# Hybrid decoder layer on one core: attention scores and linear attention rewritten with products of 128 rows and one state per pair of heads

## The chip, the cores and the metric

The kernel runs on one core of a Trainium2 chip. The metric is the device time of one execution in microseconds (us); 0.5% of it is 10 us.

## What is computed

One decoder layer over 1024 tokens of width 1024, in float32. One input projection feeds two head groups; their outputs go through one output projection, and a mixture of 32 experts with 4 chosen per token follows. The change touches the two head groups alone:

```python
# (A) window attention: 8 query heads, 2 key heads, width 64, blocks of 128 tokens with the block before
s = einsum('bnqhgd,bnkhd->bnhgqk', qb, kb) * scale        # masked, softmax with a sink, times v

# (B) linear attention: 4 heads, key width 64, value width 128, chunks of 64 tokens
glog = log_sigmoid(ga @ w_gla_gate_up + b_gla_gate) / 16
b = cumsum(g, axis=2); b_last = b[:, :, -1:]; b_mid = b[:, :, C // 2 - 1:C // 2]
A = einsum('bnihd,bnjhd->bnhij', q * exp(b - b_mid), k * exp(b_mid - b))     # causal inside a chunk
o = einsum('bnhij,bnjhv->bnihv', A, v)
kv = einsum('bnjhd,bnjhv->bnhdv', k * exp(b_last - b), v)
state = exp(b_last) * state + kv                                             # chunk after chunk
o = o + einsum('bnihd,bnhdv->bnihv', q * exp(b), states)                     # the state before the chunk
```

## The kernel before

The program is written with tiles and pools; a scheduler sets the order of the instructions on each engine, which the engines then keep. It has three stages. The first (to about 165 us) normalises the tokens and makes queries, keys and gate inputs for all 1024 tokens; `pieces_of_k` (L359 to L366) writes the float16 key `kk`, twice over 128 partitions for each key head, and its remainder `kl` (L365), in 64 partitions for each key head. The second, the mixer, is the loop over t = 0 to 7 of `layer_kernel` (from L675), each pass over a tile of 128 tokens, that is two chunks of 64. The third (router, experts, output) begins with `project_out`.

In pass t, SP loads pieces of the output weights (`wo`, L684 and L687) and of `w_ada` (L634); GpSimd reduces the latter (`ada_half`, L636 to L643). `project` (L149 to L151 inside it) makes values and output gates with 96 float16 products of 256 columns; they depend on nothing in the pass, and the scheduler strews them among the others as filling on TensorE. `gla_gates` (L532 to L563) makes the decay factors: one product of 16 rows (L535), a bias added by VectorE (L537), ScalarE's logarithm (L539 to L541), a running sum by a product with a triangle (L546), four tiles of exponentials (L552 to L557) and four multiplications of 256 columns (L562). `attention` makes its scores with 16 products (L466 and L467): for each of 8 heads one of 128 rows with the key and one of 64 rows with the remainder:

```python
nc.tensor.matmul(pss[g][:, a, :w], qq[:, g, i, tq], kk[:, g, tk], start=True, stop=False)
nc.tensor.matmul(pss[g][:, a, :w], qq[g * 64:(g + 1) * 64, g, i, tq],
                 kl[g * 64:(g + 1) * 64, tk], start=False, stop=True)
```

VectorE masks and reduces each head (L472). The pool `psS` has two buffers, so the scores of the second four heads wait until L472 has read those of the first. After L472 come the softmax (L476 to L486), transposes (L493) and 16 products with the values (L502). `gla` makes the chunk products (L570, 64 rows each), selects the causal part of both chunks (L573), transposes the keys (L576), then for each chunk four products of 64 by 64 (L589) and a new state (L593), and for each head one product of 128 rows with the values (L600) and one of 64 rows with the state of each chunk (L603). The second chunk's state product waits for L593. L608 to L611 normalise the result `go`, which L710 transposes.

Of the kernel before, what the change touches and what calls it, by code (L numbers as in the profile page):

```python
# [19 lines left out]
T = 1024  # L20
D = 1024
NT = 8
# [27 lines left out]
def layer_kernel(  # L50
# [110 lines left out]
    kl = midp.tile([128, T], F16, name="kl")  # L161
# [3 lines left out]
    gaT = midp.tile([16, T], F32, name="gaT")  # L165
# [6 lines left out]
    with tc.tile_pool(name="p1", bufs=1) as p1, tc.tile_pool(name="stage", bufs=4) as stage, \  # L172
# [210 lines left out]
        for t in range(NT):  # L383
# [8 lines left out]
            nc.vector.tensor_copy(gaT[:, tk], pt[:16, 0:128])  # L392
# [24 lines left out]
    with tc.tile_pool(name="p2", bufs=1) as p2, tc.tile_pool(name="wk", bufs=2) as wk, \  # L417
            tc.tile_pool(name="wos", bufs=1, side="right") as wos:
        wup = p2.tile([16, 256], F32, name="wup")
        nc.sync.dma_start(wup, w_up)  # L420
        bgb = p2.tile([128, 256], F32, name="bgb")
        nc.sync.dma_start(bgb, bcast_row(b_gla_gate, 256))
# [9 lines left out]
        nc.vector.tensor_scalar(amask[:, 128:256], io, 0.0, -1e30, op0=OP.is_gt, op1=OP.mult)  # L432

# [12 lines left out]
        S0 = wk.tile([128, 2, 128], F32, name="Sn", bufs=4)  # L446
        nc.vector.memset(S0, 0.0)
        Sst = [S0]
# [4 lines left out]
        def attention(t, ao):  # L453
# [4 lines left out]
            for i2 in range(2):  # L458
# [3 lines left out]
                for a in range(2):  # L462
                    for g in range(2):
# [3 lines left out]
                        nc.tensor.matmul(pss[g][:, a, :w], qq[g * 64:(g + 1) * 64, g, i, tq],  # L467
                                         kl[g * 64:(g + 1) * 64, tk], start=False, stop=True)
# [63 lines left out]
        def gla_gates(t):  # L532
# [9 lines left out]
            nc.vector.scalar_tensor_tensor(zb, zb, 0.0, az, op0=OP.min, op1=OP.subtract)  # L542
            pb = psS.tile([128, 2, 256], F32, name="pss")
            pbv = pb[:, 0, :].rearrange("p (a n) -> p a n", a=2)
            for a in range(2):
                nc.tensor.matmul(pbv[:, a, :], zb[:, a * 128:(a + 1) * 128], tri16, start=True, stop=True)  # L546
            bT = wk.tile([128, 4, 64], F32, name="bT", bufs=1)
            bf = bT.rearrange("p a n -> p (a n)")
            nc.scalar.activation(bf, pb[:, 0, :], AF.Copy)
            ee = wk.tile([128, 4, 256], F32, name="ee")  # L550
            ev = ee.rearrange("p e (a n) -> p e a n", a=4)
            nc.vector.tensor_tensor(ev[:, 0], bT, bT[:, :, 31:32].to_broadcast([128, 4, 64]), op=OP.subtract)  # L552
            nc.vector.tensor_tensor(ev[:, 2], bT[:, :, 63:64].to_broadcast([128, 4, 64]), bT, op=OP.subtract)
            nc.scalar.activation(ee[:, 1, :], ee[:, 0, :], AF.Exp, scale=-1.0)
            nc.scalar.activation(ee[:, 0, :], ee[:, 0, :], AF.Exp)
            nc.scalar.activation(ee[:, 2, :], ee[:, 2, :], AF.Exp)
            nc.scalar.activation(ee[:, 3, :], bf, AF.Exp)  # L557
            e3 = wk.tile([128, 4], F32, name="e3")
            nc.vector.tensor_copy(e3, ev[:, 3, :, 63])
# [3 lines left out]
            return qk, e3  # L563

        def gla(t, qk, e3, gv, sgg, go):
            A = am[t % 2]
            pas = [psS.tile([128, 2, 128], F32, name="pss") for _ in range(2)]
            for h in range(4):
                bs = slice(64 * (h % 2), 64 * (h % 2) + 64)
                nc.tensor.matmul(pas[h % 2][:, h // 2, :], qk[bs, 1, h // 2, :], qk[bs, 0, h // 2, :],  # L570
                                 start=True, stop=True)
            for par in range(2):
                nc.vector.copy_predicated(A[:, par::2, :], triu[:, None, :].to_broadcast([128, 2, 128]), pas[par])  # L573
            pk = psT.tile([128, 4, 128], F32, name="pt")
            for a in range(2):
                nc.tensor.transpose(pk[:, a, :], qk[:, 2, a, :], identf)  # L576
            k2 = wk.tile([128, 2, 128], F32, name="k2", bufs=1)
            nc.scalar.activation(k2, pk[:, 0:2, :], AF.Copy)
            k2f = k2.rearrange("p a n -> p (a n)")
            Sc = []  # L580
            for cch in range(2):
                Sc.append(Sst[0])
                if t == NT - 1 and cch == 1:
                    break
                cs = slice(64 * cch, 64 * cch + 64)
                pkv = psS.tile([128, 2, 128], F32, name="pss")
                for h in range(4):
                    bs = slice(64 * (h % 2), 64 * (h % 2) + 64)
                    nc.tensor.matmul(pkv[bs, h // 2, :], k2f[cs, h * 64:(h + 1) * 64],  # L589
                                     gv[cs, h * 128:(h + 1) * 128], start=True, stop=True)  # L590
                Sn = wk.tile([128, 2, 128], F32, name="Sn", bufs=4)
                for a in range(2):
                    nc.vector.scalar_tensor_tensor(Sn[:, a, :], Sst[0][:, a, :], e3[:, 2 * a + cch:2 * a + cch + 1],  # L593
                                                   pkv[:, a, :], op0=OP.mult, op1=OP.add)
                Sst[0] = Sn
            pos2 = [psO.tile([128, 2, 128], F32, name="po") for _ in range(2)]
            for h in range(4):
                bs = slice(64 * (h % 2), 64 * (h % 2) + 64)
# [878 lines left out]
```

## Time and profile before

| | |
|---|---|
| median of 3 runs | 2007.46 us (2006.25 to 2015.17) |
| profiled execution | 2014.17 us, of which the span in the trace is 2012.4 us |
| TensorE matmul busy | 1847.7 us, 92% of the span |
| VectorE / ScalarE / GpSimd busy | 1545.2 / 1303.8 / 991.0 us |
[...]

Busy time of TensorE counts a product until its modelled end, so neighbours overlap; the distance between two starts is what a product costs in a stream. A float32 product leaves two records, so "x8" there is four products. Idle time stands in brackets, with what ended it.

### The profile page before, as it was taken

The page shows a single profiled execution, that of the slowest core. Times are in us where ns is not written, and L with a number is a line of the kernel's source. Part 1 is how long each engine was busy: PE and PEld are TensorE (multiplying, and loading weights), DVE is VectorE, ACT ScalarE, POOL GpSimd, SP SyncE. Part 2 cuts the span into 40 slices and gives each one's busy share as a digit, 9 for nine tenths or more (in the row PEclk, how much of TensorE's full clock was granted, in tenths as well). Part 3 has the DMA queues.
Part 4 walks back from the last instruction along what each step waited for, and adds up shares of the span by engine and source line. Part 5 has one row for each costly group of instructions (what it writes and reads, how often), then busy time and mean ns, then how long its engine had stood idle before and what let it go on. Part 6 is the DMA issues. An engine that isn't in the chain of part 4 may idle for free. (4 is left out here: it accounts for less than half of the span.)

```text
span 2012.4 us, 55645 instructions
## 1 busy us (share of the span) xinstructions
PE 1847.7 (92%) x22929; PEld 1583.9 (79%) x22929; DVE 1545.2 (77%) x2518; ACT 1303.8 (65%) x2248; POOL 991.0 (49%) x986
## 2 busy tenths in 40 slices
PE   7999999989778999999999999999999999999980
PEld 3456767655468999999999997779889998999970
DVE  6823655666759998998999996679787978989863
ACT  5523444443447787787787885668677868968860
POOL 2204757635636455554574663336453534754442
PEclk8999989999869999999999999999999999999985
DMA  8512323243299999999999998589888989999983
GB/s 277 165 46 74 85 80 93 83 141 126 100 317 329 354 363 320 340 360 325 350 347 358 366 341 289 198 309 342 313 284 293 362 274 338 361 317 344 323 262 105
DMA packets 296773, 525.94 MB, mean 261 GB/s; under 512 B 19071, under 2 KB 79753, under 8 KB 296482
## 3 DMA queue, kind: packets, MB, share of 16 engines
q1 hardware_dynamic: 277824, 476.40, 68.2%
q0 software_dynamic: 17392, 41.72, 8.7%
q8 instruction: 181, 2.97, 0.6%
q10 hardware_dynamic: 1298, 4.21, 0.5%
q14 instruction: 78, 0.64, 0.1%
HBM read 482.50 MB, written 39.76 MB: 260 GB/s over the span
## 5 line engine op out<-in xcount | busy, mean ns | idle before, releaser
L169 DVE SCALAR_TENSOR_TENSOR el<-st,eh 128x1024 f16<-128x1024 f32 x768 | 934.8, 1239 | 92.4 <-ACT eh L168 88.4
L168 ACT ACTIVATE eh<-st 128x1024 f16<-128x1024 f32 x768 | 794.5, 1055 | 240.3 <-PE pu L150 121.5
L149 PE MATMUL pu<-xTh,eh 128*128 128x232 f16 (+31 forms) x4096 | 779.2, 231 | 9.2 <-DVE lin L1122 4.7
L151 PE MATMUL pu<-xTh,el 128*128 128x232 f16 (+31 forms) x4096 | 778.4, 230 | 5.8 <-issue 5.7
L150 PE MATMUL pu<-xTl,eh 128*128 128x232 f16 (+31 forms) x4096 | 778.1, 230 | 4.1 <-issue 3.9
L150 PEld LDWEIGHTS <-eh 128*128 128x128 f16 x6080 | 595.0, 99 | 38.8 <-issue 16.7
L149 PEld LDWEIGHTS <-eh 128*128 128x128 f16 x6080 | 592.9, 98 | 29.7 <-issue 7.7
L151 PEld LDWEIGHTS <-el 128*128 128x128 f16 x6080 | 592.4, 98 | 29.8 <-issue 7.9
L1125 POOL CAST aTh<-lin 128x232 f16<-128x232 f32 (+31 forms) x256 | 296.7, 1159 | 495.5 <-DVE lin L1124 457.3
L149 PE MATMUL pyv<-aTh,eh 128*128 128x232 f16 (+30 forms) x1984 | 375.2, 231 | 5.9 <-ACT yT L1152 4.5
L150 PE MATMUL pyv<-aTl,eh 128*128 128x232 f16 (+30 forms) x1984 | 374.8, 231 | 3.2 <-issue 3.2
L151 PE MATMUL pyv<-aTh,el 128*128 128x232 f16 (+30 forms) x1984 | 374.9, 231 | 0.8 <-issue 0.8
L1126 POOL TENSOR_TENSOR aTl<-lin,aTh 128x232 f16<-128x232 f32 (+31 forms) x256 | 255.3, 997 | 20.7
L1122 DVE TENSOR_SCALAR lin<-pu,bt 128x232 f32<-128x232 f32 (+31 forms) x256 | 109.7, 428 | 76.8 <-PE pu L151 58.0
L1167 POOL DMA_INDIRECT yacc<-yo,tokI x52 | 94.6, 1819 | 113.7 <-ACT yo L1164 107.1
L636 POOL TENSOR_TENSOR st<-st,sil 128x512 f32<-128x512 f32 x64 | 68.4, 1069 | 153.6 <-DVE ee L562 96.7
L1118 ACT ACTIVATE gl<-pu,bt 128x232 f32<-128x232 f32 (+31 forms) x256 | 98.0, 383 | 62.9 <-PE pu L151 36.6
L1123 DVE SCALAR_TENSOR_TENSOR lin<-lin,bt,sg 128x232 f32<-128x232 f32 (+31 forms) x256 | 104.5, 408 | 18.1 <-ACT sg L1120 4.2
L1120 ACT ACTIVATE sg<-gl,c 128x232 f32<-128x232 f32 (+31 forms) x256 | 107.9, 421 | 1.0
L1080 POOL DMA_INDIRECT xg<-h2d,gatI x50 | 70.8, 1416 | 43.4 <-DVE gcol L1243 21.1
L1124 DVE SCALAR_TENSOR_TENSOR lin<-gl,lin 128x232 f32<-128x232 f32 (+31 forms) x256 | 83.6, 326 | 4.3
L1072 PE MATMUL pxh<-identh,xg 128*128 128x128 f16 (+27 forms) x848 | 55.6, 206 | 19.7 <-DMA xg<-h2d,gat 11.7
(402 smaller groups left out, 2501.4 us busy)
## 6 DMA issues: line engine op xcount, KB each, us to landing
st<-in_w_mlp_dram SPq DMA_DIRECT2D x384, 1024.0 KB
st<-in_w_ada_dram SPq DMA_DIRECT2D x64, 256.0 KB
xt<-in_x_dram SPq DMA_DIRECT2D x16, 512.0 KB
st<-in_w_ada_dram SPq DMA_DIRECT2D x16, 512.0 KB
st<-in_w_in_dram SPq DMA_DIRECT2D x7, 1024.0 KB
x1d<-xt SPq DMA_DIRECT2D x8, 512.0 KB
h2d<-h2s SPq DMA_DIRECT2D x8, 512.0 KB
yacc<-yi ACTq DMA_DIRECT2D x8, 512.0 KB
```

The costliest lines, as they stand in the source:

```text
L149: nc.tensor.matmul(ps, sh, mh, start=first, stop=False)
L150: nc.tensor.matmul(ps, sh, ml, start=False, stop=False)
L151: return nc.tensor.matmul(ps, sl, mh, start=False, stop=last)
L168: return (nc.scalar.activation(dh, src, AF.Copy, scale=SW), nc.vector.scalar_tensor_tensor(dl, src, SW, dh, op0=OP.mult, op1=OP.subtract))
L169: nc.vector.scalar_tensor_tensor(dl, src, SW, dh, op0=OP.mult, op1=OP.subtract))
L1118: nc.scalar.activation(gl, pu[0], AF.Relu, scale=-SG, bias=bc(0, j))
L1120: sgs.append(nc.scalar.activation(sg, gl, AF.Sigmoid, scale=-1.702 * INV / SG, bias=c7))
L1122: nc.vector.tensor_scalar(lin, pu[1], bc(1, j), bc(2, j), op0=OP.max, op1=OP.min)
L1123: nc.vector.scalar_tensor_tensor(lin, lin, bc(3, j), sg, op0=OP.add, op1=OP.mult)
L1125: nc.gpsimd.tensor_copy(aTh[:, j, :], lin)
L1126: lows.append(nc.gpsimd.tensor_tensor(aTl[:, j, :], lin, aTh[:, j, :], op=OP.subtract))
L1167: end["dma"] = nc.gpsimd.indirect_dma_start(out=yacc, out_offset=bass.IndirectOffsetOnAxis(ap=si(b)[:m, :], axis=0), in_=yo[:m, :], in_off ...
```

## The change

The remainder `kl` gets its own copy in all 128 partitions for each key head, so all 16 score products have 128 rows (L470). The bias of the gates becomes a row of the weights `wup`, met by a row of ones in `gaT`; VectorE's addition goes, and the product has 128 rows. In `gla_gates` the state factors are written per chunk, so that a tile's two chunks share one state step: the keys of the first chunk and the queries of the second are also multiplied by the other chunk's whole decay. In `gla` there are four extra products of 64 columns (L585: second chunk's queries with first chunk's keys), copied beside the causal part (L590); one product of 128 rows and 256 columns for each pair of heads with the state `S` (L593), which holds the two heads in diagonal blocks; two products of 256 columns for the new state in place of eight (L606), and none in the last pass. The head results lie in one PSUM tile in place of two.

```diff
-    kl = midp.tile([128, T], F16, name="kl")
+    kl = midp.tile([128, 2, T], F16, name="kl")
-    gaT = midp.tile([16, T], F32, name="gaT")
+    gaT = midp.tile([128, T], F32, name="gaT")
+    nc.gpsimd.memset(gaT, 0.0)
+    nc.gpsimd.memset(gaT[32:33, :], 1.0)
...
-                nc.vector.scalar_tensor_tensor(kl[hi, ts], ps[hi], INV * SX, kk[hi, g, ts],
-                                               op0=OP.mult, op1=OP.subtract)
+                for at in (hi, lo):
+                    nc.vector.scalar_tensor_tensor(kl[at, g, ts], ps[hi], INV * SX, kk[hi, g, ts],
+                                                   op0=OP.mult, op1=OP.subtract)
...
-        wup = p2.tile([16, 256], F32, name="wup")
-        nc.sync.dma_start(wup, w_up)
-        bgb = p2.tile([128, 256], F32, name="bgb")
-        nc.sync.dma_start(bgb, bcast_row(b_gla_gate, 256))
+        wup = p2.tile([128, 256], F32, name="wup")
+        nc.vector.memset(wup, 0.0)
+        nc.sync.dma_start(wup[0:16, :], w_up)
+        nc.sync.dma_start(wup[32:33, :], bcast_row(b_gla_gate, 256, 1))
...
-                        nc.tensor.matmul(pss[g][:, a, :w], qq[g * 64:(g + 1) * 64, g, i, tq],
-                                         kl[g * 64:(g + 1) * 64, tk], start=False, stop=True)
+                        nc.tensor.matmul(pss[g][:, a, :w], qq[:, g, i, tq], kl[:, g, tk], start=False, stop=True)
...
-            zb = wk.tile([128, 256], F32, name="zb", bufs=1)
-            nc.vector.tensor_add(zb, pz[:, 0, :], bgb)
-            nc.scalar.activation(az, zb, AF.Abs)
+            nc.scalar.activation(az, pz[:, 0, :], AF.Abs)
...
-            for n, src in enumerate((gqT, gkT, gkT, gqT)):
+            for n, src in ((0, gqT), (1, gkT)):
                 nc.vector.tensor_tensor(qk[:, n], src[:, :, tk], qk[:, n], op=OP.mult)
+            for n, src, c in ((4, gkT, 0), (2, gqT, 1)):
+                for cch, to in ((c, 3), (1 - c, n)):
+                    cs = slice(64 * cch, 64 * cch + 64)
+                    nc.vector.tensor_tensor(qk[:, to, :, cs], src[:, :, t * 128 + 64 * cch:t * 128 + 64 * cch + 64],
+                                            qk[:, n, :, cs], op=OP.mult)
+                cs = slice(64 * c, 64 * c + 64)
+                nc.vector.tensor_tensor(qk[:, n, :, cs], qk[:, 3, :, cs],
+                                        e3[:, :, 1 - c:2 - c].to_broadcast([128, 2, 64]), op=OP.mult)
+            nc.vector.tensor_tensor(e4, e3[:, :, 0], e3[:, :, 1], op=OP.mult)
...
+                nc.tensor.matmul(pa[:, 0:128], qk[bs, 1, h // 2, :], qk[bs, 0, h // 2, :], start=True, stop=True)
+                nc.tensor.matmul(pa[:, 128:192], qk[bs, 3, h // 2, :], qk[bs, 3, h // 2, 64:128],
                                  start=True, stop=True)
...
+                nc.vector.tensor_copy(A[0:64, par::2, 64:128], pas[par][0:64, :, 128:192])
+            pos4 = psO.tile([128, 4, 128], F32, name="po")
+            for a in range(2):
+                nc.tensor.matmul(pos4[:, 2 * a:2 * a + 2, :].rearrange("p h n -> p (h n)"), qk[:, 2, a, :], S[:, a, :],
+                                 start=True, stop=False)
+                for h in (2 * a, 2 * a + 1):
+                    nc.tensor.matmul(pos4[:, h, :], A[:, h, :], gv[:, h * 128:(h + 1) * 128],
+                                     start=False, stop=bool(h % 2))
+            if t < NT - 1:
...
+                for a in range(2):
+                    nc.tensor.matmul(pkv[:, a, :], k2[:, a, :], gv[:, a * 256:(a + 1) * 256], start=True, stop=True)
+                for a in range(2):
+                    for hh in range(2):
+                        bs, ns = slice(64 * hh, 64 * hh + 64), slice(128 * hh, 128 * hh + 128)
+                        nc.vector.scalar_tensor_tensor(S[bs, a, ns], S[bs, a, ns], e4[bs, a:a + 1],
+                                                       pkv[bs, a, ns], op0=OP.mult, op1=OP.add)
```

The scheduler's order changes with it. On VectorE in pass t = 5, before, the first head's reduction (L472, two rows each) stands in the middle of the decay factors (`ee`):

```order
L712 SCALAR_TENSOR_TENSOR hTl<-pt,ggc,hTh 128x4x128
L552 TENSOR_TENSOR ee<-bT 128x256
L553 TENSOR_TENSOR ee<-bT 128x256
L559 COPY e_3203<-ee 128x4
L472 ISA sm,mx<-pss,amask 128x256
L472 ISA mx 128x1
L562 TENSOR_TENSOR ee<-gqT,ee 128x256
L562 TENSOR_TENSOR ee<-gkT,ee 128x256 x2
L562 TENSOR_TENSOR ee<-gqT,ee 128x256
L528 SCALAR_TENSOR_TENSOR vg_3309<-pb,vg_3309 128x512
L472 ISA sm,mx<-pss,amask 128x256
```

The same place with the change, where L474 is the reduction and L560 to L573 are the decay factors and their new pieces:

```order
L554 TENSOR_TENSOR ee<-ee 128x256
L563 TENSOR_TENSOR ee<-gkT,ee 128x256
L567 TENSOR_TENSOR ee<-gkT,ee 128x2x64 x2
L563 TENSOR_TENSOR ee<-gqT,ee 128x256
L560 COPY e_3171<-ee 128x4
L567 TENSOR_TENSOR ee<-gqT,ee 128x2x64
L570 TENSOR_TENSOR ee<-ee,e_3171 128x2x64
L567 TENSOR_TENSOR ee<-gqT,ee 128x2x64
L570 TENSOR_TENSOR ee<-ee,e_3171 128x2x64
L573 TENSOR_TENSOR e_3181<-e_3171 128x2
L527 TENSOR_SCALAR vg_3283<-vg_3283 128x512
L474 ISA sm,mx<-pss,amask 128x256
```

No reduction now comes before the last decay factor. On TensorE the scores move to match: in pass 5, before, the first eight score products follow L546 at once and 30 projection products stand between them and the next four; now 34 projection products stand between L546 and the first eight, and 8 behind them.

On TensorE at the end of pass 5, before, the states and the results of the last two heads come last, between the last projection products and the next pass:

```order
L150 LDWEIGHTS hTh
L150 MATMUL pb<-wvl_1329,hTh 128x256
L589 MATMUL pss<-vg_3258,k_3476 64x128 x8
L151 LDWEIGHTS hTl
L151 MATMUL pb<-wvh_1328,hTl 128x256
L603 MATMUL po<-Sn,ee 64x128 x2
L600 MATMUL po<-vg_3258,am_1386 128x128
L603 MATMUL po<-Sn,ee 64x128 x2
L600 MATMUL po<-vg_3258,am_1386 128x128
L603 MATMUL po<-Sn,ee 64x128 x2
```

With the change the results of all four heads (L593 and L596) stand earlier, among the transposes (L495) and the products with the values (L504) of the attention:

```order
L495 MATMUL pt<-identf,sm 128x128 x5
L593 MATMUL po<-S,ee 128x256
L596 MATMUL po<-vg_3232,am_1392 128x128 x2
L593 MATMUL po<-S,ee 128x256
L504 MATMUL po<-vv,pT 128x64 x8
L495 MATMUL pt<-identf,sm 128x128 x4
L596 MATMUL po<-vg_3232,am_1392 128x128 x2
```

The new state's two products (L606) stay at the end of the pass, and no product of the pass waits for the state they make.

## Rows read from the trace of the kernel before

**Rows 1.** The page: span, busy time, and granted clock in 40 slices.
```profile
span 2012.4 us, 55645 instructions
...
PE 1847.7 (92%) x22929; PEld 1583.9 (79%) x22929; DVE 1545.2 (77%) x2518; ACT 1303.8 (65%) x2248; POOL 991.0 (49%) x986
...
PEclk8999989999869999999999999999999999999985
```
**Rows 2.** Windows: start:end, length, busy PE, PEld, DVE, ACT, POOL, clock, DMA share, GB/s.
```profile
164.00:420.00 256.00, 242.19 (x1859) 175.88 (x1857) 147.82 (x419) 117.28 (x374) 163.58 (x261) 0.97 0.32 92
...
650.00:2000.00 1350.00, 1271.56 (x18749) 1196.35 (x18746) 1149.94 (x1539) 1005.70 (x1529) 684.55 (x598) 0.98 0.94 319
```
**Rows 3.** Timeline of TensorE in pass 5 (start, duration, instruction): scores, projections, transposes.
```profile
331.39 0.68 PE L546 MATMUL pss<-tri,zb 128*128 128x128 f32 x4 [0.59 <-DVE zb L542]
331.91 0.27 PE L466 MATMUL pss<-kk,qq 128*128 128x256 f16 x1
...
333.61 0.28 PE L150 MATMUL pb<-wvl,hTh 128*128 128x256 f16 x1
...
333.84 0.27 PE L149 MATMUL pb<-wvh,hTh 128*128 128x256 f16 x1
333.95 0.27 PE L150 MATMUL pb<-wvl,hTh 128*128 128x256 f16 x1
...
342.39 0.38 PE L493 MATMUL pt<-identf,sm 128*128 128x128 f32 x2
342.61 0.27 PE L150 MATMUL pb<-wvl,hTh 128*128 128x256 f16 x1
```
**Rows 4.** Waits: total us, times, longest; weight loads of L467.
```profile
PEld L467 <- issue: 11.2, 30, 2.4
```
**Rows 5.** Timeline of TensorE in pass 5: linear attention, and L502 between.
```profile
339.90 0.71 PE L570 MATMUL pss<-ee 64*128 64x128 f32 x4
340.55 0.28 PE L149 MATMUL pb<-wvh,hTh 128*128 128x256 f16 x1
...
343.99 1.10 PE L502 MATMUL po<-vv,pT 128*128 128x64 f32 x8
344.93 0.72 PE L493 MATMUL pt<-identf,sm 128*128 128x128 f32 x5
345.49 0.39 PE L600 MATMUL po<-vg,am 128*128 128x128 f32 x2
345.80 0.43 PE L603 MATMUL po<-Sn,ee 64*64 64x128 f32 x2
346.16 0.28 PE L151 MATMUL pb<-wvh,hTl 128*128 128x256 f16 x1
...
353.74 0.68 PE L589 MATMUL pss<-vg,k 64*64 64x128 f32 x16
354.35 0.28 PE L151 MATMUL pb<-wvh,hTl 128*128 128x256 f16 x1
354.84 0.43 PE L603 MATMUL po<-Sn,ee 64*64 64x128 f32 x4 [0.21 <-DVE Sn L593]
...
356.78 0.69 PE L535 MATMUL pss<-wup,gaT 16*128 16x256 f32 x2
```
**Rows 6.** Timeline of TensorE: the two longest waits of the mixer, passes 3 and 7.
```profile
270.20 0.27 PE L466 MATMUL pss<-kk,qq 128*128 128x256 f16 x1 [2.04 <-DVE mx L472]
...
420.15 0.84 PE L710 MATMUL pt<-identf,go 128*128 128x128 f32 x3 [2.28 <-DVE go L611]
```
**Rows 7.** Windows, columns as in rows 2: the stretch around the wait of pass 3.
```profile
268.00:284.00 16.00, 13.96 (x72) 9.53 (x70) 7.51 (x29) 5.34 (x19) 9.84 (x15) 0.68 0.19 56
```
**Rows 8.** Timeline of VectorE in pass 3: start of the decay factors, first reduction.
```profile
261.61 0.41 DVE L542 SCALAR_TENSOR_TENSOR zb<-zb,az 128x256 f32<-128x256 f32 x1
...
268.79 0.41 DVE L472 CUSTOM_DVE_ANT_0 sm<-pss,amask 128x256 f32<-128x256 f32 x1
```
**Rows 9.** The instructions of line L562: shortest/median/longest ns, first and last start.
```profile
L562 DVE TENSOR_TENSOR ee<-gqT,ee x16: 407/422/1281, 170.5 to 397.0; 128x256 f32<-128x256 f32 x16
```

More of the change, by code (lines that the diff above doesn't have):

```diff
@@ L391, in layer_kernel @@
             nc.tensor.transpose(pt[:16, 0:128], ga[:, t, :], identf)
[L392 removed]
+            nc.vector.tensor_copy(gaT[0:16, tk], pt[:16, 0:128])
         for base, dst, sc in ((768, gqT, INV / 8), (1024, gkT, INV)):
@@ L445, in layer_kernel @@
             am.append(a)
-        S0 = wk.tile([128, 2, 128], F32, name="Sn", bufs=4)
-        nc.vector.memset(S0, 0.0)
-        Sst = [S0]
+        S = p2.tile([128, 2, 256], F32, name="S")
+        nc.gpsimd.memset(S, 0.0)
         for i in range(2):
@@ L545, in gla_gates @@
             for a in range(2):
-                nc.tensor.matmul(pbv[:, a, :], zb[:, a * 128:(a + 1) * 128], tri16, start=True, stop=True)
-            bT = wk.tile([128, 4, 64], F32, name="bT", bufs=1)
-            bf = bT.rearrange("p a n -> p (a n)")
+                nc.tensor.matmul(pbv[:, a, :], az[:, a * 128:(a + 1) * 128], tri16, start=True, stop=True)
+            ee = wk.tile([128, 5, 256], F32, name="ee")
+            ev = ee.rearrange("p e (a n) -> p e a n", a=4)
+            bT, bf = ev[:, 2], ee[:, 2, :]
@@ L566, in gla @@
+            e4 = wk.tile([128, 2], F32, name="e4")
+            nc.vector.tensor_tensor(e4, e3[:, :, 0], e3[:, :, 1], op=OP.mult)
+            return ee, e4
+        def gla(t, ee, e4, gv, sgg, go):
             A = am[t % 2]
-            pas = [psS.tile([128, 2, 128], F32, name="pss") for _ in range(2)]
+            qk = ee.rearrange("p e (a n) -> p e a n", a=2)
+            pas = [psS.tile([128, 2, 256], F32, name="pss") for _ in range(2)]
             for h in range(4):
                 bs = slice(64 * (h % 2), 64 * (h % 2) + 64)
-                nc.tensor.matmul(pas[h % 2][:, h // 2, :], qk[bs, 1, h // 2, :], qk[bs, 0, h // 2, :],
+                pa = pas[h % 2][:, h // 2, :]
+                nc.tensor.matmul(pa[:, 0:128], qk[bs, 1, h // 2, :], qk[bs, 0, h // 2, :], start=True, stop=True)
+                nc.tensor.matmul(pa[:, 128:192], qk[bs, 3, h // 2, :], qk[bs, 3, h // 2, 64:128],
@@ L575, in gla @@
+            pos4 = psO.tile([128, 4, 128], F32, name="po")
             for a in range(2):
[L576 to L591, printed above, removed]
-                for a in range(2):
-                    nc.vector.scalar_tensor_tensor(Sn[:, a, :], Sst[0][:, a, :], e3[:, 2 * a + cch:2 * a + cch + 1],
-                                                   pkv[:, a, :], op0=OP.mult, op1=OP.add)
-                Sst[0] = Sn
@@ L596, in gla @@
-            pos2 = [psO.tile([128, 2, 128], F32, name="po") for _ in range(2)]
-            for h in range(4):
-                bs = slice(64 * (h % 2), 64 * (h % 2) + 64)
-                po = pos2[h % 2][:, h // 2, :]
-                nc.tensor.matmul(po, A[:, h, :], gv[:, h * 128:(h + 1) * 128], start=True, stop=False)
-                for cch in range(2):
-                    cs = slice(64 * cch, 64 * cch + 64)
-                    nc.tensor.matmul(po[cs, :], qk[bs, 3, h // 2, cs], Sc[cch][bs, h // 2, :],
-                                     start=False, stop=True)
+                nc.tensor.matmul(pos4[:, 2 * a:2 * a + 2, :].rearrange("p h n -> p (h n)"), qk[:, 2, a, :], S[:, a, :],
+                                 start=True, stop=False)
@@ new lines, in gla @@
+                for h in (2 * a, 2 * a + 1):
+                    nc.tensor.matmul(pos4[:, h, :], A[:, h, :], gv[:, h * 128:(h + 1) * 128],
+                                     start=False, stop=bool(h % 2))
+            if t < NT - 1:
+                pk = psT.tile([128, 4, 128], F32, name="pt")
+                for a in range(2):
+                    nc.tensor.transpose(pk[:, a, :], qk[:, 4, a, :], identf)
+                k2 = wk.tile([128, 2, 128], F32, name="k2", bufs=1)
+                nc.scalar.activation(k2, pk[:, 0:2, :], AF.Copy)
+                pkv = psS.tile([128, 2, 256], F32, name="pss")
+                for a in range(2):
[5 more added lines that the diff above has]
+                                                       pkv[bs, a, ns], op0=OP.mult, op1=OP.add)
@@ L691, in layer_kernel @@
             ao = wk.tile([128, 8, 64], F32, name="ao", bufs=1)
-            qk, e3 = gla_gates(t)
+            gates = gla_gates(t)
             gv, sgg = project(t, row)
@@ L706, in layer_kernel @@
             go = wk.tile([128, 4, 128], F32, name="go", bufs=1)
-            gla(t, qk, e3, gv, sgg, go)
+            gla(t, *gates, gv, sgg, go)
             pt = psT.tile([128, 4, 128], F32, name="pt")
```

24 lines of the change are left out of this document (10 added, 14 removed).

## The prediction

> **What bounds the kernel now.** I read the page first, for where time passes, then windows by stage, then the timeline of TensorE through one pass of the mixer, then its waits. [...] The change touches the mixer, from 164 to 420 us. There TensorE works for 242.2 of 256 us at a mean granted clock of 0.97, while VectorE is busy for 148, ScalarE for 117 and GpSimd for 164 us, and the transfers take a third of their engines' time [rows 2]. So the mixer lasts as long as TensorE's stream of products plus 13.8 us of waits. The experts follow it and run at a DMA share of 0.94 [rows 2]; their weights are not read during the mixer, so whatever the mixer gains moves the rest forward whole.
>
> **The scores.** A projection product, 128 rows and 256 columns of float16, follows another at 0.11 us (333.84 to 333.95) [rows 3]. The first eight score products of pass 5, of the same 256 columns, take 331.91 to 333.61, that is 1.70 us or 0.21 each [rows 3]. They alternate between 128 and 64 rows. Two other rows say that the alternation is what costs. The weight loads of L467 are not hidden: 30 of them stand idle for 11.2 us, 0.37 each [rows 4]. And transposes of 128 rows, of another type and put between projections, cost no extra: two in 0.22 us (342.39 to 342.61) [rows 3]. With all sixteen at 128 rows I price them at 0.11: 16 x 0.11 = 1.76 in place of 3.40 us, 1.64 less in each of passes 1 to 7, 11.5 us. Pass 0 has half the columns and no row here; between nothing and 1.6 us I take 0.8. Sum: 12.3 us less.
>
> [...]
>
> **The linear attention, per pass.** Four steps, all by rows 5.
> - Four extra products of 64 columns. In float32 and 128 rows such a product costs 0.235 us (four from 343.99 to 344.93), one of 64 rows and 128 columns 0.325 (two from 339.90 to 340.55) [rows 5]. Ends: half of 0.325, and 0.325. I take 0.235, the nearest in columns: 0.94 more (0.65 to 1.30).
> - The results. Before, a head costs 0.67 us (0.31 for L600, 0.36 for its two state products; 345.49 to 346.16), and this stands twice; the other two heads run from the end of the last projection, 354.35 + 0.11, to 356.78, 2.32 with a wait of 0.21 that I count below [rows 5]. Together 3.45 without the wait. After, four products at 0.31 and two of 256 columns in float32, for which no row stands: at most twice 0.31, at least the 0.44 that four float16 products of 256 columns need [rows 3, 5]. I take 0.5: 2.24, so 1.2 less (1.0 to 1.3).
> - The states. Eight products of 64 by 64 take 0.61 us (353.74 to 354.35), 0.08 each where one of 128 rows takes 0.31, so they run beside each other [rows 5]. Two of 256 columns at 0.5 are 1.0: 0.4 more (0.25 to 0.65). This part speaks against the change.
> - The gate product has 128 rows for 16 and the same columns: nothing, or a tenth less.
>
> Sum per pass: 0.94 - 1.2 + 0.4 = 0.14 more, 1.1 in eight; the last pass drops its states and two transposes (some 0.5 less, and the 0.4 is not paid). So 0.2 more in all, which I call nothing, with ends of 6 us less and 6 more. The linear attention is a wash; the scores carry the gain.
>
> **The waits.** The wait for the new state, 0.21 us [rows 5], stands in all eight passes: 1.7 us go, since the results now read the state of the pass before. The results stand earlier in the order, so the chain behind them (squares, root, `go`, transposes) starts earlier, and the longest wait of the mixer, 2.28 us for `go` in pass 7 [rows 6], should go too. Without the bias addition on VectorE (0.4 us and a hand-over) the gates reach L546 earlier; the wait there, 0.59 in pass 5 [rows 3], goes in the passes that have it: 1 us. What is late next are the second four heads' scores. They wait for VectorE's reduction of the first (L472 of before), and the new order puts all decay factors ahead of it. There are four half-width multiplications, two half-width scalings and a tiny product more, two full multiplications and the addition less. By columns alone this is some 0.5 us more per pass before the first reduction, at the full price of each instruction (0.42) [rows 9] 1.8 more. TensorE brings 34 + 8 projections and eight scores, 42 x 0.11 + 0.87 = 5.5 us, after L546. VectorE needs 6 to 7 us there. So I expect waits of half a microsecond to one in each of seven passes, some 5 us, where before one pass had 2.04 [rows 6] and the others at most half of that, some 3 in all: 2 us more.
>
> [...]
>
> Work I cost at nothing: the second copy of `kl` (four more instructions on VectorE, before 165 us), because TensorE has projections queued there and VectorE waits for it; the two memsets on GpSimd, idle then; the copies beside the causal part, hidden by projections up to about 0.4 us a pass, beyond which they would delay the softmax; the bias transfer, now one row. GpSimd and SP keep their work. GpSimd is busy for 164 of 256 us [rows 2] and would bind only if a pass fell well under 27 us; I expect 28 from 30.
>
> **The sum.** 12.3 + 0 + 1.7 + 2.3 + 1.0 - 2.0 is 15.3 us less on waits and products at the high clock. In the mixer the clock was at 0.97, so 3% of 256 us or 8 us were lost to the low level, and fewer long waits give back perhaps a third: 2.5. I forecast 18 us less. The profiled execution of 2014.2 us becomes 1996; it lay 6.7 above the median, so the median goes from 2007.5 to **1989.5 us**.
>
> **Rivals.**
> - *VectorE's chain takes the gain and more (slower).* In pass 3 the chain from the gates' end (261.61 + 0.41) to the first reduction took 6.8 us [rows 8], since multiplications that meet GpSimd's take up to 1281 ns for a median 422 [rows 9]. TensorE waited 2.04 us [rows 6], and the 16 us around it ran at a clock of 0.68 [rows 7]: 16 x 0.32 = 5.1 us lost, 7.2 in all. Now the chain is longer in every pass. Waits near 2 us decide, because after this one the clock fell. If five to seven of seven passes do this, it costs 36 to 50 us, less the 7 paid already and the 18 gained: 11 to 25 slower, about 2025. Three or four such passes eat the gain: 2004 to 2011. For it speaks the order; against it that before only one of seven passes did so, and that the reductions now follow each other closely. 0.08 for the slower form, 0.10 for the even one.
> - *The scores stay at 0.21 us (the change does not do what it is for).* If the price is that of accumulating two products in one place and not of the alternation, 12.3 of the 18 us fall away: 2002. Rows 4 speak against it. [...] 0.10.
> - *The clock stays high throughout the mixer.* All 8 us come back and not a third: 1984 or, with the float32 products at their low ends, 1978. For it speaks that the longest waits go; 0.12.
>
> **The numbers.** The forecast has 0.60: 1982 to 1997. Half a per cent, 10 us, is about what a measurement of this kernel can tell from no change. Faster by more than that takes the forecast and the high clock, 0.72; the same takes this even form and the scores that stay, 0.20; slower 0.08. The range for 8 in 10 runs from 1976 to 2006: it leaves out the slower rival and the ends of the others.
>
> **What would show it.** Right: score products 0.11 us apart; a pass of about 28 us where it was 30; no wait of L600's successors for the state; the eight products of L589 replaced by two of 0.4 to 0.6; the stretch after 420 us unchanged but shifted. Wrong: waits of TensorE for the reduction (L474 in the new numbering) of 2 us and more in several passes, with the clock at 0.5 behind them; score products still 0.2 apart; float32 products of 256 columns at over 0.62; the gain of the mixer not found again at the end.

## The result, and the profile after

The median is 1986.0 us (4 runs, 1980.7 to 1991.8) where the kernel before has 2011.3 beside it: a ratio of 0.987 (95% interval 0.983 to 0.992), some 25 us less. Seven more runs, taken later, gave 1985.7 beside 2009.7: 0.990 (0.987 to 0.994). The forecast was 1989.5, 18 us less, in a range of 1976 to 2006.

The page after, against [rows 1]: TensorE is busy for 34 us less, VectorE and GpSimd for 13 and 16 more, and no slice of the mixer (the fourth to the eighth) is below 0.9, where one was.

```profile
span 1978.6 us, 55425 instructions
...
PE 1813.5 (92%) x22803; PEld 1587.7 (80%) x22803; DVE 1558.1 (79%) x2568; ACT 1305.4 (66%) x2247; POOL 1007.2 (51%) x989
...
PEclk9999999999699999999999999999999999999985
```

Four stages of the two profiled executions, in us: the first gate product begins at 164.7 before and at 160.7 after; the mixer, from there to the last transpose of `go`, takes 256.4 and 230.0; from there to the first transpose of the experts' tokens 150.0 and 150.7; from there to the end 1441.3 and 1437.2. So 26 of the 34 us between these two executions lie in the mixer. The 4 ahead of it are not the change's: a later run (`e3_pairs`) that leaves the first stage as it was began its mixer at 160.4, and the granted clock of the first stage was 0.95 before and 0.98 after.

Nor are all of the 26. The end of the mixer is filled with products of the output projection, 512 columns of float16, 0.215 us apart. One of their three groups, by the list of TensorE's groups in the mixer, before and then after:

```profile
L149 PE MATMUL pb<-woh,hTh 128*128 128x512 f16 x16 | 6.1, 381 | 0.0
```

```profile
L149 PE MATMUL pb<-woh,hTh 128*128 128x512 f16 x10 | 3.8, 379 | 0.0
```

With a single one more before, that is 49 and 30. Nineteen of them, 4.1 us, now stand behind the mixer. The stage behind it grew by 0.7 us only; its granted clock was 0.86 before and 0.89 after, by estimate (0.03 of 150 us) worth some 4 us in these two executions.

The timeline of TensorE after, pass 5, in the columns of [rows 3]. L469 and L470 are scores, L584 the chunk products, L585 the cross products, L593 and L596 the results, L606 the new state, L537 the next pass's gate product (L717 transposes `go`):

```profile
303.38 1.13 PE L606 MATMUL pss<-vg,k 128*128 128x256 f32 x4
304.35 0.27 PE L717 MATMUL pt<-identf,go 128*128 128x128 f32 x1
304.46 0.60 PE L537 MATMUL pss<-wup,gaT 128*128 128x256 f32 x2
304.89 0.27 PE L717 MATMUL pt<-identf,go 128*128 128x128 f32 x1
...
311.31 0.27 PE L469 MATMUL pss<-kk,qq 128*128 128x256 f16 x1
311.42 0.27 PE L470 MATMUL pss<-kl,qq 128*128 128x256 f16 x1
...
315.31 0.27 PE L469 MATMUL pss<-kk,qq 128*128 128x256 f16 x1 [2.09 <-DVE mx L474]
...
317.47 0.49 PE L584 MATMUL pss<-ee 64*128 64x128 f32 x2
317.80 0.33 PE L585 MATMUL pss<-ee 64*128 64x64 f32 x2
317.97 0.44 PE L584 MATMUL pss<-ee 64*128 64x128 f32 x2
318.24 0.33 PE L585 MATMUL pss<-ee 64*128 64x64 f32 x2
318.51 0.28 PE L150 MATMUL pb<-wvl,hTh 128*128 128x256 f16 x1
...
324.35 0.60 PE L593 MATMUL po<-S,ee 128*128 128x256 f32 x2
324.78 0.61 PE L596 MATMUL po<-vg,am 128*128 128x128 f32 x4
325.23 0.60 PE L593 MATMUL po<-S,ee 128*128 128x256 f32 x2
325.66 0.55 PE L504 MATMUL po<-vv,pT 128*128 128x64 f32 x4
...
333.33 0.60 PE L537 MATMUL pss<-wup,gaT 128*128 128x256 f32 x2
```

A pass takes 28.9 us (304.46 to 333.33) where this one took 30.0. Scores stand 0.11 us apart. A group of two chunk and two cross products takes 1.04 (317.47 to 318.51) where two chunk products took 0.65 [rows 5]. A result product of 256 columns in float32 takes 0.43 (324.35 to 324.78), one of 128 columns 0.225 (two to 325.23), the two state products 0.97 (303.38 to 304.35). The wait for the state [rows 5] is gone. The waits for L474, the reduction, are what TensorE has now; by the list of its waits in the mixer (total us, times, longest):

```profile
PE pss L469 <- DVE mx L474: 8.4, 7, 2.5
PE pss L546 <- DVE az L542: 3.9, 4, 2.9
```

Before, the same two came to 3.8 and 2.1 us:

```profile
PE pss L466 <- DVE mx L472: 3.8, 4, 2.0
PE pss L546 <- DVE zb L542: 2.1, 2, 1.5
```

Beside them `go` in pass 7 (2.3, [rows 6]), the state (1.8) and L670 in pass 2 (1.9) cost 6.0; of these 0.8 is left, the last one's.

### The profile page after: what moved, and what is told of

The parts are those of the page before. It is cut to its first block, busy times and chain, and to the rows that moved or that the text cites. A ratio compares the mean times of both kernels' runs of the same rounds, so it can differ in the third digit from the quotient of the medians.

```text
span 1978.6 us, 55425 instructions
## 1 busy us (share of the span) xinstructions
PE 1813.5 (92%) x22803; PEld 1587.7 (80%) x22803; DVE 1558.1 (79%) x2568; ACT 1305.4 (66%) x2247; POOL 1007.2 (51%) x989
## 5 line engine op out<-in xcount | busy, mean ns | idle before, releaser
L150 PEld LDWEIGHTS <-eh 128*128 128x128 f16 x6080 | 595.1, 99 | 42.0 <-issue 20.2
L1133 POOL TENSOR_TENSOR aTl<-lin,aTh 128x232 f16<-128x232 f32 (+31 forms) x256 | 271.2, 1060 | 20.6
L1171 ACT ACTIVATE yo<-pxy,gcol 128x512 f32<-128x512 f32 (+26 forms) x104 | 70.3, 678 | 5.8 <-DMA yacc<-yo,tokI 5.8
```

What stands on the lines that cost most here:

```text
L150: nc.tensor.matmul(ps, sh, ml, start=False, stop=False)
L1133: lows.append(nc.gpsimd.tensor_tensor(aTl[:, j, :], lin, aTh[:, j, :], op=OP.subtract))
```

## The experiments

The two theories at the start: the gain is the sum of the product prices (A), or it comes from the new order of the engines, by waits and clock (B). All 12 kernels are compared with the kernel before on the same chip; its medians there were 2010.6, 2009.7 and 2008.7. For the reading, each profiled mixer (first gate product to last transpose of `go`) is split: its waits on TensorE; what it lost to the low clock, by estimate the length times one minus the granted clock (two digits, so within 1.3 us); and what remains, the products. At a granted clock of 0.50 (196 to 198 us of the change) the projections stood 0.21 us apart where they stand 0.11 apart at 1.00.

| kernel | median, runs | ratio, 95% interval | mixer | waits | low clock | products |
|---|---|---|---|---|---|---|
| before | 2009 to 2011 | | 256.4 | 13.1 | 7.7 | 235.6 |
| the change | 1986.0, 4 | 0.983 to 0.992 | 230.0 | 14.0 | 2.3 | 213.8 |
| `after_again` | 1985.7, 7 | 0.987 to 0.994 | 234.0 | 14.4 | 4.7 | 214.8 |
| `e1_scores_bias` | 2009.1, 10 | 0.996 to 1.003 | 249.1 | 21.1 | 2.5 | 225.6 |
| `e2_linear_alone` | 2023.4, 10 | 1.002 to 1.008 | 257.5 | 17.8 | 15.4 | 224.2 |
| `e3_pairs` | 2018.2, 10 | 1.001 to 1.006 | 265.8 | 22.0 | 21.3 | 222.5 |
| `e4_pairs_linear` | 2001.7, 10 | 0.992 to 0.998 | 242.8 | 17.3 | 9.7 | 215.8 |
| `e5_scores_first` | 2010.2, 11 | 0.998 to 1.003 | 257.6 | 24.7 | 33.5 | 199.4 |
| `e6_scores_bias_first` | 1998.5, 11 | 0.992 to 0.999 | 241.1 | 15.4 | 7.2 | 218.4 |
| `e7_linear_first` | 2021.0, 11 | 1.003 to 1.009 | 268.9 | 19.5 | 32.3 | 217.1 |
| `e8_remainder_64` | 1997.5, 11 | 0.992 to 0.997 | 235.1 | 6.2 | 2.4 | 226.4 |
| `e9_gate_copy` | 2008.2, 11 | 0.998 to 1.003 | 243.4 | 22.8 | 7.3 | 213.3 |
| `e10_split_behind` | 1985.1, 5 | 0.986 to 0.992 | 228.8 | 14.9 | 0.0 | 213.9 |
| `e11_bias_row` | 2017.6, 11 | 1.001 to 1.005 | 259.2 | 14.3 | 10.4 | 234.6 |

A low stretch that holds a wait counts it in two columns, so where the low clock is over 20 us the products come out too small; there only the first five columns are read. The products hold those of the output projection too, 49 of them before and in `e1`, `e3` and `e11`, 30 in the change, its repeat, `e2` and `e8`, and 14 to 37 in the others; between 49 and 30 lie 4.1 us that are moved and not saved. The four columns on the right are of one profiled execution, and some of these lie far from their median: `e2` 13 us and `e8` 11 below, `e7` 13 and `e1` 10 above.

**The two halves alone.** `e1_scores_bias` is the kernel before with the diff's lines on `kl`, L470, `gaT`, `wup` and the addition; `e2_linear_alone` is the change with these lines as they were.

```diff
-                        nc.tensor.matmul(pss[g][:, a, :w], qq[g * 64:(g + 1) * 64, g, i, tq],
-                                         kl[g * 64:(g + 1) * 64, tk], start=False, stop=True)
+                        nc.tensor.matmul(pss[g][:, a, :w], qq[:, g, i, tq], kl[:, g, tk], start=False, stop=True)
...
-            zb = wk.tile([128, 256], F32, name="zb", bufs=1)
-            nc.vector.tensor_add(zb, pz[:, 0, :], bgb)
```

> Of the change, the score products of 128 rows and the bias row alone; the linear attention as before. Theory A (TensorE's stream of products sets the mixer, and the change's gain is the sum of its product prices): score products 0.11 us apart, 12 us less for them, and 2 to 5 more from a wait at L546 that goes and from the clock: 12 to 17 us less than before, 1990 to 1996 beside a median before of 2007. Theory B (the gain of the whole change comes from the new order of VectorE and TensorE, that is from waits and clock): the products are 0.11 us apart but the waits for the reduction grow, and under 8 us are won, 1999 or more.

> Of the change, the linear attention alone; scores at 128 and 64 rows and the bias addition as before. The prediction had this part at nothing (2007). Theory A, with the prices now read after the change (a product of 256 columns in float32 at 0.43 us in place of 0.5, one of 64 columns at 0.2 in place of 0.235): results 1.7 us less in a pass, cross products 0.8 more, states 0.4 more, the wait for the state gone: 0.7 us less in a pass, 5 to 6 in all, and up to 4 from the clock: 5 to 10 us less than before, 1997 to 2002; with the run of the scores alone it adds up to the whole change within 5 us. Theory B (order and clock carry the whole gain): 15 us less or more, or nothing, and the sum with the scores alone misses the whole by over 8 us.

Alone, the first gives nothing and the second 13 us more; together they give 24 less. The products add up, though: 10.0 and, without the 4.1 that are moved, 7.3 us less than before, 17.3 in all, where the change has 17.7 and 16.7. Theory A holds for the products, B for waits and clock, and both times lie nearer to B's: the first half has 8 us more of waits, the second 5 more and twice the loss to the low clock (15.4 for 7.7). (In the first, 249.1 is 7 us better than before, and its profiled execution then spent 1455 us on the experts where before has 1441. Its ten runs fall into three at 1995 to 1998 and seven at 2007 to 2022. Where the upper seven lose it isn't settled.) In the second the clock fell behind four of its waits for the reduction, for 3 to 10 us each. The timeline of TensorE in pass 3, and the window behind the wait, in the columns of [rows 2]:

```profile
267.93 0.27 PE L466 MATMUL pss<-kk,qq 128*128 128x256 f16 x1 [2.86 <-DVE mx L472]
```

```profile
268.00:280.00 12.00, 12.00 (x60) 8.79 (x60) 6.47 (x21) 4.97 (x19) 9.52 (x14) 0.57 0.23 66
```

**The price of a score product.** `e3_pairs` changes the order of the scores in the kernel before, `e4_pairs_linear` makes the same edit to the change and keeps the remainder at 64 rows.

```diff
+                    hi = [nc.tensor.matmul(pss[g][:, a, :w], qq[:, g, i, tq], kk[:, g, tk], start=True, stop=False)
+                          for g in range(2)]
+                    with tc.issue_after(hi[1].ins):
+                        for g in range(2):
+                            nc.tensor.matmul(pss[g][:, a, :w], qq[g * 64:(g + 1) * 64, g, i, tq],
+                                             kl[g * 64:(g + 1) * 64, tk], start=False, stop=True)
```

> The kernel before with its score products in another order and nothing else: the two products of 128 rows of a pair of heads first, then their two remainders of 64 rows, so that TensorE changes between 128 and 64 rows half as often. Before, four such products take 0.85 us. Theory A (each change of the row count costs, 0.1 us): two changes in place of four, 0.64 us a group, or 0.53 if the two remainders, which lie in different halves, run beside each other: 56 groups of four in passes 1 to 7, and some gain in pass 0, is 11 to 12 (0.64) up to 18 us (0.53) less than half of that each, that is 5 to 9 us less in all, as 28 groups hold the 16 products of seven passes. Theory C (a product of 64 rows, or one that adds to the product before it, costs 0.3 us by itself): 0.85 us stays and the time is that of before, within 3 us.

> The whole change, but the remainders of the scores stay at 64 rows, ordered in pairs: two products of 128 rows, then the two remainders in different halves. Theory A: four products at 0.64 us in place of 0.44, 0.2 x 28 groups, 5 to 6 us more than the change; if the remainders run beside each other (0.53 or less), within 3 us of it, and at 0.35 or less 2 to 3 us faster. Theory C: 0.85 us a group, 11 to 12 us more than the change.

The timeline of TensorE in `e4_pairs_linear`, pass 5:

```profile
320.26 0.38 PE L467 MATMUL pss<-kk,qq 128*128 128x256 f16 x2
320.58 0.28 PE L471 MATMUL pss<-kl,qq 64*128 64x256 f16 x2
320.80 0.39 PE L467 MATMUL pss<-kk,qq 128*128 128x256 f16 x2
```

Four products take 0.54 us (320.26 to 320.80), where the alternating four take 0.85 and four of 128 rows 0.44. So by these rows a change of the row count costs about 0.1 us ((0.85 - 0.44) / 4), and the two remainders, in different halves, take the time of one: 0.28 us from the first's start to the second's end, where the two of 128 rows take 0.38 and one remainder alone took 0.28 before. 0.11 x 3 + 0.1 x 2 = 0.53. The products of 128 rows accumulate as well and stand 0.11 us apart, so accumulating has no price of its own here; the rival that the scores stay at 0.21 falls. The times went the other way: 8 us more than before, and 16 more than the change for products 1 to 2 us dearer. In both the mixer shows more waits than before (17.3 and 22.0 us for 13.1) and a greater loss to the low clock (9.7 and 21.3 for 7.7).

**Once more, and the reductions first.** In `e5_scores_first` the scores and L474 of the change stand in a block of high priority, so that VectorE reduces before or between its multiplications; `e6_scores_bias_first` and `e7_linear_first` do so in the two halves.

```diff
+                with tc.high_priority():
                     for a in range(2):
...
                     for g in range(2):
                         for a in range(2):
                             h = 2 * (2 * i2 + a) + g
```

> The change as it is, once more, on one chip with the three runs that follow. The two parts alone had given 0 and 12 us more, in medians of 10 runs, and the change 25 us less, in 4 runs. Theory D (the parts need each other: each alone leaves TensorE with waits of 2 us for the reduction in nearly every pass and, where the scores still have 64 rows, with long stretches at the low clock behind them; together they avoid the low clock): 1981 to 1992 again, 20 us or more below the kernel before, with at most 3 us lost to the low clock between 160 and 420 us. Rival E (the 4 runs were lucky ones): 1995 or more, with a low clock behind the waits for the reduction in passes 3, 5 and 7.

> The change, with the scores and their reductions ranked ahead of the decay factors, so that the eight reductions of a pass come before or between VectorE's multiplications. Theory D: the waits for the reduction in passes 3, 5 and 7 (1.8 to 2.5 us) and those of half a microsecond go, 8 us in all, unless the chunk products, now later, wait as long for their factors; 1976 to 1982, 4 to 10 us less than the change. Rival F (waits are moved, not removed: the transposes or the chunk products then wait for VectorE): as the change within 3 us.

> The scores of 128 rows and the bias row alone, with the reductions ranked ahead of the decay factors. Without that rank its waits for VectorE came to 16.7 us in passes 0 to 6, 8.0 more than before, and took what the products had won, 12.3. Theory D: the waits fall to some 6 us and 10 of the 12 come through: 1996 to 2001 where the kernel before has 2010. Rival F: the waits come back elsewhere, 2005 to 2012.

> The linear attention alone, with the reductions ranked ahead of the decay factors. Without that rank it had 15 us of waits in passes 0 to 6 and lost 15 us to the low clock, beside a stream of products 8.9 us shorter. Theory D: without the waits the clock stays high and the shorter stream shows: 1996 to 2004, 15 to 25 us less than without the rank. Rival G (the low clock comes from the score products of 64 rows themselves, whatever the waits): the clock still falls in two or more passes, and it stays above 2008.

The change's gain stands (theory D), but not with the clock as D had it: the same program fell to the low level behind two waits at which it had not fallen the first time (0.98 over the mixer, 0.99 the first time). In `e6_scores_bias_first` 11 us come through, which is D's number; but the waits shrink from 21.1 to 15.4 only, those for VectorE in passes 0 to 6 from 16.7 to 12.0 where D had 6, so D's reason is borne out in part. In `e5_scores_first`, F holds, and worse: the waits move to the products with the values, and the clock falls behind them (0.87 over the mixer). The timeline and the window around the first:

```profile
180.86 1.97 PE L505 MATMUL po<-vv,pT 128*128 128x64 f32 x8 [3.42 <-DVE pT L502]
```

```profile
178.00:192.00 14.00, 11.14 (x47) 9.84 (x48) 6.62 (x14) 4.22 (x10) 10.60 (x15) 0.52 0.40 114
```

This wait cost 3.4 us and, by estimate, another 6.7 (14 x 0.48) of clock. `e7_linear_first` has seven low stretches (0.88 over the mixer) and is no faster than without the rank, which is G's number. Two of them, G's case, stand behind no wait over 0.4 us, but behind products of one column (L660, the sums of `w_ada`; seven in pass 2, eight in pass 6), which keep TensorE busy for 1.5 to 1.7 us; the scores that follow have 64-row remainders.

**Which part the others need.** `e8_remainder_64` is the change with `kl` and L467 of before (the first three lines of the diff of the halves, reversed). `e11_bias_row` is the kernel before with the bias row alone (the last two lines of that diff, with `gaT` and `wup`). `e9_gate_copy` is the change with one line put in ahead of `az`:

```diff
+            nc.vector.tensor_copy(pz[:, 0, :], pz[:, 0, :])
```

> The whole change but the score products with the remainder, which keep their 64 rows in the order of before. Theory H (what the parts give each other goes through the score rows: with 64 rows the waits for the reduction bring the clock down for 10 us and more): 11.5 us of products and 10 or more of clock come back, 2008 to 2020. Rival I (it goes through the bias row, which lets the gates reach VectorE earlier and so changes the order of both engines): only the products come back and little clock, 1997 to 2003.

> The whole change, with one more pass of VectorE over the gate product, a copy in place, where the bias addition had stood; what is computed stays the same. The prediction gave the removed addition 1.0 us. Theory H: 0.4 us and a hand-over in each pass, part of it beside projections: 1987 to 1993. Rival I: the order of before comes back with its waits, 1998 or more.

> The kernel before with the bias as a row of the gate product alone. The prediction's step: the wait at L546 shrinks and 1 us goes; 2006 to 2011 where the kernel before has 2010. Rival I: the new order alone changes waits and clock by 6 us or more, in either direction.

With everything else of the change in place, the score rows are worth 11.8 us in the medians (1997.5 to 1985.7), about the price of their products. The profiled mixers differ by 1 to 5 us only: `e8` has 12 us more of products there and 8 us fewer waits, and where its median loses the rest was not placed. The linear attention is worth 23 (2009.1 to 1985.7), and the one pass of VectorE over the gate product that the bias row spares is worth 22.5 (2008.2 to 1985.7), though no product differs between `e9_gate_copy` and the change. The bias row alone costs 9. So rival I is right for the bias row, and theory H was wrong: without the score rows the change had the fewest waits of all, 6.2 us. VectorE's timeline shows how the copy acts. In `e9_gate_copy`, pass 5 (gate product at 313.02), the copy stands in VectorE's queue behind the updates of the state (L611):

```profile
312.90 1.43 DVE L611 SCALAR_TENSOR_TENSOR S<-S,e,pss 64x128 f32<-64x128 f32 x4 [0.22 <-PE pss L607]
314.36 0.43 DVE L538 COPY pss<-pss 128x256 f32<-128x256 f32 x1
...
316.14 0.42 DVE L543 SCALAR_TENSOR_TENSOR az<-pss,az 128x256 f32<-128x256 f32 x1 [0.56 <-ACT az L542]
...
324.39 0.41 DVE L474 CUSTOM_DVE_ANT_0 sm<-pss,amask 128x256 f32<-128x256 f32 x1
```

The same chain of the change, pass 5 (gate product at 304.46):

```profile
306.52 0.42 DVE L542 SCALAR_TENSOR_TENSOR az<-pss,az 128x256 f32<-128x256 f32 x1
...
314.49 0.41 DVE L474 CUSTOM_DVE_ANT_0 sm<-pss,amask 128x256 f32<-128x256 f32 x1
```

`az` follows the gate product by 3.1 us with the copy and 2.1 without, the first reduction by 11.4 and 10.0. TensorE's wait at that reduction is 3.67 us in `e9_gate_copy` and 2.09 in the change; over the mixer 14.7 and 8.4. Of the 22 us, the profiled mixers account for 9 to 13; the rest was not placed.

**The wait at L546 in pass 1.** ScalarE's timeline of the change: its part of the split of the output weights stands ahead of the gates and waits for its transfer.

```profile
190.67 0.63 ACT L170 ACTIVATE woh<-wo 128x512 f16<-128x512 f32 x1 [4.18 <-DMA wo<-in_w_out_dram]
191.21 0.37 ACT L539 ACTIVATE az<-pss 128x256 f32<-128x256 f32 x1
```

```diff
-                    nc.scalar.activation(pT[:, :2 * nk, :], pt[:, :2 * nk, :], AF.Copy)
+                    ex = nc.scalar.activation(pT[:, :2 * nk, :], pt[:, :2 * nk, :], AF.Copy)
...
-            with tc.issue_after(rec.ins):
+            with tc.issue_after(rec.ins), tc.issue_after(ex.ins):
```

> The change, with ScalarE's part of the split of the output weights (L170) put behind the pass's last copy of the transposes, as VectorE's part already stands behind the softmax. After the change ScalarE's split of pass 1 stood ahead of that pass's gates and waited 4.2 us for its transfer, TensorE then 2.9 to 3.3 us at L546 with the clock down for 4 us. Theory J (that wait is on the path): it goes, and with it the low clock there: 3 to 6 us less than the change, 1980 to 1983. Rival F (waits are moved, not removed): as the change within 2 us.

The wait at L546 goes, and the mixer's clock is 1.00 throughout. But 14.9 us of waits remain: those for the reduction grow from 8.4 to 9.3, and pass 7 waits 2.7 for `go` again. The mixer is 1 to 5 us shorter, the median 1985.1 where the change has 1986.0 and 1985.7. That is F's number; no version here is shown to beat the change.

## Why the prediction was right, and where not

The time and the direction were right, the sum less so: the linear attention saved what the sum didn't have, and the waits for VectorE took more than it allowed, so that two errors cancelled in part. That the forecast came within 4 us of the median is luck to that extent. By its terms, in us:

| term | predicted | measured |
|---|---|---|
| scores | -12.3 | -13.2 by rows |
| linear attention, products | 0 (6 either way) | about -7 by rows, -4 to -8 by mixers |
| wait for the state; wait for `go` | -1.7; -2.3 | -1.8; -2.3 |
| wait at L546 | -1.0 | +1.8 |
| waits for the reduction | +2.0 | +4.6 |
| wait at L670 in pass 2 | not priced | -1.1 |
| low clock | -2.5 | -5.4, -3.0 in the second profile |

- *The scores.* Sixteen at 0.11 save 1.65 in seven passes, as forecast. Pass 0, where between 0 and 1.6 was open, saved 1.65: its products of 128 columns went from 0.16 to 0.056 us apart (176.51 to 177.62 before and 172.54 to 172.93 after, for seven steps).
- *The linear attention, "a wash".* This step failed. Per pass the results cost 1.76 where 3.45 stood, 1.7 less and not 1.2; the four cross products 0.78 and not 0.94; the states 0.36 more, as priced; the gate product 0.43 for 0.62. That is 0.74 less a pass and not 0.14 more. The low end of 0.44 for a product of 256 columns in float32, four in float16, was the author's estimate, which no row before shows; after, such a product took 0.43. The price of 0.31 for a 128-row product was read between products of 64 rows [rows 5]; between products of 128 rows it is 0.225. That it held a change of the row count is inferred from these two prices and not shown by a run of its own. The mixers agree in sign and roughly in size. Without the 4.1 us that are moved, the linear attention has 7.3 us fewer products in `e2_linear_alone`, 7.7 in the change against `e1_scores_bias`, and 4.1 in `e8_remainder_64` against `e11_bias_row`, each within some 2.5. Over the whole change the rows promise 20.2 us and the mixers show 16.7 to 17.7. One reading was wrong without harm: 345.80 to 346.16 [rows 5] is one state product (two records) and not a head's two; the pass has eight, and the 3.45 us hold them all.
- *The bias addition.* It was priced by the one wait it stood at, 1 us. Its worth lies elsewhere, in a chain that ends at the reduction 10 us later; with the rest of the change it is 22 us in the medians (`e9_gate_copy`), 9 to 13 of them seen in the profiled mixers.
- *The waits for the reduction.* They grew, as forecast, but by 4.6 us and not by 2.0. From the end of `az` to the first reduction VectorE took 7.6 us in pass 5 (306.94 to 314.49), not 6 to 7. The prediction counts half a microsecond more by columns, but the pieces that it lists come out even (six of 128 columns against three of 256). What it left out of this term is GpSimd, which it has among the rivals alone. VectorE's and then GpSimd's timeline of the change, pass 5:

```profile
311.22 1.12 DVE L570 TENSOR_TENSOR ee<-ee,e 128x128 f32<-128x128 f32 x1
...
313.20 1.03 DVE L573 TENSOR_TENSOR e<-e 128x2 f32<-128x2 f32 x1
```

```profile
311.11 1.08 POOL L643 TENSOR_TENSOR st<-st,sil 128x512 f32<-128x512 f32 x1 [1.11 <-DMA st<-in_w_ada_dram]
...
313.18 1.04 POOL L643 TENSOR_TENSOR st<-st,sil 128x512 f32<-128x512 f32 x1
```

  In pass 4, with GpSimd idle beside them, the same two instructions took 0.28 and 0.15 us; here each ends when GpSimd's multiplication does or shortly after. This lengthening (some 2.2 us with the second L570, which took 0.81) is as large as the wait of 2.09 us that follows. No run took GpSimd's work away, so how much of the 8.4 us of waits is its doing stays open.
- *The slower rival.* In the change, VectorE's chain took 4.6 us and not the gain. In `e2_linear_alone` and `e9_gate_copy` it takes the gain, as the rival said, though in the second by waits (22.8 us) more than by the clock (7.3). So the mechanism was right and its distance was small: one VectorE instruction more in the chain. Its point of decision, waits near 2 us, was wrong: behind 1.79, 2.09 and 2.49 us (passes 3, 5, 7) the clock stayed at 1.00.
- *Work costed at nothing.* "Whatever the mixer gains moves the rest forward whole" holds for the change by its figures (150.7 and 1437 us against 150.0 and 1441), but the first pair agrees by chance: 4.1 us of products more against some 4 us less lost to the low clock, by estimate. `e1_scores_bias` shows that a single execution can differ by 14 us in the experts.

## What to carry to other kernels

Price a product by a row whose neighbours are like those it will have: the scores next to others of another row count carried some 0.1 us for the change between them. With TensorE's stream made shorter, the chain on VectorE that runs beside it became the next bound here (the waits for the reduction went from 3.8 to 8.4 us), and an instruction there was worth more than its length: eight copies of 0.43 us (`e9_gate_copy`) brought some 8.5 us of waits and, by estimate, 3 to 5 us lost to the low clock. So test the parts of a change with the others in place: the linear attention alone cost 13 us and the bias row alone 9. The score rows were not run without the bias row.

## What the hardware showed beyond that

The same wait did not always bring the clock down. In the change TensorE waited 2.09 us in pass 5 and went on at a granted clock of 1.00; in the second profile of the same program it waited 1.95 us at the same place. The windows around each, of the change:

```profile
314.00:322.00 8.00, 6.19 (x48) 4.91 (x48) 7.45 (x26) 2.98 (x10) 6.34 (x11) 1.00 0.24 68
```

and of `after_again`, where the wait ended at 317.93:

```profile
317.00:325.00 8.00, 7.07 (x46) 5.73 (x46) 6.13 (x25) 2.89 (x10) 6.39 (x10) 0.79 0.25 71
```

A long wait was not needed either. In `e8_remainder_64` (0.99 over the mixer) the clock fell at 226 us, with 0.3 us of waiting ahead of it, behind the eight one-column products of pass 2 (two records each):

```profile
223.57 0.68 PE L546 MATMUL pss<-tri,az 128*128 128x128 f32 x4 [0.32 <-DVE az L542]
224.09 1.84 PE L659 MATMUL pss<-onesf,adac 128*128 128x1 f32 x16
225.80 0.27 PE L150 MATMUL pb<-wvl,hTh 128*128 128x256 f16 x1
```

The same eight products stand in passes 4 and 6 as well, where the clock stayed up, and in three passes of the change, where it fell behind none of them (1.00 in all its mixer but 194 to 200 us). So they are not enough by themselves.

How long the clock stayed low differed with what came next: 3 to 4 us in the mixer of the change (0.72, 0.50 and 0.93 in the three stretches of 2 us from 194), its repeat and `e8_remainder_64`, each time ahead of projections or 128-row scores (0.11 us apart at 1.00); up to 10 us in `e2_linear_alone` (0.57 in 268 to 280), whose scores alternate; 7 to 17 us in `e5_scores_first` (0.52 in 178 to 192 and in 212 to 228), ahead of 64-column products and transposes in float32. That the work behind a wait decides its price fits these rows, but was not tested by itself, and one stretch speaks against it: in `e9_gate_copy` (0.97 over the mixer) the clock was low for 7 us around a wait of 3.69 us for `az` in pass 1 (it ended at 196.82), ahead of the same projections as in the change.
